# Reading the stationary weights of split fp32 matmuls with a step of two elements

## The chip, the cores and the metric

The kernel runs on one core of a Trainium2 chip. The metric is the device time of one execution in microseconds (us), the median of several runs. Engines are named as in the profile: PE is TensorE's matmul, PEld TensorE's loading of the stationary operand (the weights that stay in the array while the moving operand streams past), DVE is VectorE, ACT ScalarE, POOL GpSimd, SP the engine whose queue issues the DMAs.

## The reference: what is computed

Two layers of an encoder over 256 positions of width 2048, everything in fp32. Layer 0 mixes tokens with a gated MLP, layer 1 with grouped-query attention; after each comes a gated FFN with a convolution of width 3. A vector `c` gives shifts, scales and gates.

```
for i in range(2):
    sh1, sc1, gt1, sh2, sc2, gt2 = split(silu(c) @ w_ada[i] + b_ada[i], 6)
    h = rmsnorm(x, g_norm[i, 0]) * (1 + sc1) + sh1
    y = gmlp(h) if i == 0 else gqa(h)        # 2048->4096, 2048->2048 / 2048->3072, 2048->2048
    x = x + gt1 * y
    h = rmsnorm(x, g_norm[i, 1]) * (1 + sc2) + sh2
    a = conv3(h @ f_w_up[i])                 # 2048 -> 11264
    g, val = split(a, 2)
    x = x + gt2 * ((gelu(g) * val) @ f_w_down[i])   # 5632 -> 2048
return rmsnorm(x, g_final)
```

## The kernel before

Activations lie transposed in SBUF: 128 features on the partitions, 256 positions along them. Every weight is streamed once from HBM through SP's queue, in runs of up to 128 x 2048 fp32 (`raw_tile`). To multiply in TensorE's fast fp32 format (fp32r) without losing fp32's accuracy, each operand is split in two: `hi` is the value rounded to fp32r, `lo` the rest. For weights `weight()` does this in pieces of `HW` = 1024 columns: ACT writes `hi` (line 186), VectorE writes `lo` (line 187). Activations are split into `hhi`/`hlo` (`make_h`) or `fhi`/`flo` (`split_f`); their rows are `S + STEP` = 264 elements apart, of which 256 are used, so that the rows begin at staggered addresses.

`weight()` returns a function `cols(c, n)`, which gives the `hi` and `lo` views of n columns from column c. There are two kinds of use:

- `prod_b` takes blocks of 128 columns as the *stationary* operand (`cols(c, P)`) and the 256 positions of an activation as the moving one. It issues three matmuls, `hi` x `xhi`, `hi` x `xlo`, `lo` x `xhi`, all through line 203; before each of them TensorE loads the 128 columns. Its outputs are named pu and po (gated MLP), pw (attention's output), pfa, pfc and pf (FFN up), pd (FFN down).
- The products pv, pk and pq take 512 columns of weights as the *moving* operand and an activation as the stationary one.

TensorE executes its matmuls in program order; loops over output blocks are outside, loops over the 128-blocks of the reduction inside, accumulating in PSUM. While it works on one run of weights, SP, ACT and VectorE prepare the next ones (five buffers each of raw runs, `hi` and `lo`). VectorE also computes the vector-matrix product with `w_ada` (`ada`, line 138) between its other work, and the convolution. The order of all engines is made by a scheduler when the program is built.

The host lays the weights out for this before the launch (`_layout`): the 128 columns of block 0, then those of block 1, and so on.

Of the kernel before, what the change touches and what calls it, by code (L numbers as in the profile page):

```python
# [15 lines left out]
P = 128  # L16
# [31 lines left out]
def kernel(  # L48
# [32 lines left out]
    def raw_tile(name):  # L81
        return raws.tile([P, 2048], F32, tag="raw", name=name)
# [87 lines left out]
    def pump():  # L170
        state["credit"] += state["rate"]
        while state["credit"] >= 1.0 and queue:
            state["credit"] -= 1.0
            pump_one()

    def weight(src, ncol):
        pump()
        cnt[0] += 1
        w = raw_tile(f"w{cnt[0]}")
        Q.dma_start(w[:, :ncol], src)  # L180
        his_, los_ = [], []
        for c in range(0, ncol, HW):
            n = min(HW, ncol - c)
            hi = his.tile([P, HW], F32R, tag="hi", name=f"hi{cnt[0]}_{c}")
            lo = los.tile([P, HW], F32R, tag="lo", name=f"lo{cnt[0]}_{c}")
            A.copy(hi[:, :n], w[:, c:c + n])  # L186
            V.tensor_tensor(out=lo[:, :n], in0=w[:, c:c + n], in1=hi[:, :n].bitcast(F32), op=ALU.subtract)  # L187
            his_.append(hi)
            los_.append(lo)

        ready = list(pend)
        pend.clear()
        for fn in ready:
            fn()

        def cols(c, n):
            k, o = divmod(c, HW)
            return his_[k][:, o:o + n], los_[k][:, o:o + n]

        return cols  # L200
# [503 lines left out]
def _cols(a, *lead):  # L704

    n = a.shape[-1] // P
    a = a.reshape(*a.shape[:-1], n, P)
    return np.moveaxis(a, -1, 0)


def _nblock(w):

    K, N = w.shape
    return w.reshape(K // P, P, N // P, P).transpose(2, 1, 0, 3).reshape(N // P, P, -1)


def _rope_tables():
    rows = S // 64
    row_pos = np.repeat(np.arange(rows), 64).astype(np.float32)
    col_pos = np.tile(np.arange(64), rows).astype(np.float32)  # L720
    inv = (np.float32(10000.0) ** (-np.arange(0, 64, 2, dtype=np.float32) / np.float32(64))).astype(np.float32)
    ar, ac = row_pos[:, None] * inv, col_pos[:, None] * inv
    cos = np.concatenate([np.cos(ar), np.cos(ar), np.cos(ac), np.cos(ac)], 1)
    sin = np.concatenate([-np.sin(ar), np.sin(ar), -np.sin(ac), np.sin(ac)], 1)
    f = lambda a: a.astype(np.float32).reshape(TC, P, P).transpose(1, 0, 2)
    return f(cos), f(sin)


def _layout(inp):
    a = {k: np.asarray(v) for k, v in inp.items()}  # L730
    o = {}
    o["xT"] = a["x"][0].T.reshape(NB, P, S).transpose(1, 0, 2)
    o["cT"] = _cols(a["c"][0])
    o["wada"] = a["w_ada"].transpose(0, 2, 1).reshape(DEPTH, 6 * NB, P, D)
    o["bada"] = _cols(a["b_ada"])
    o["gn"] = _cols(a["g_norm"].reshape(DEPTH * 2, D))
    o["gf"] = _cols(a["g_final"])
    win = a["a_w_in"][0]
    o["wv"] = win[:, D:].reshape(NB, P, D)
    o["wu"] = _nblock(win[:, :D])  # L740
    o["gv"] = _cols(a["a_g_v"][0])
    o["wsT"] = a["a_w_s"][0].transpose(2, 0, 1).reshape(P, NB * P)
    o["bs"] = a["a_b_s"][0].reshape(NB * P)
    o["wout"] = _nblock(a["a_w_out"][0])
    wq = a["b_w_qkv"][0]
    o["wqkv0"] = np.concatenate([wq[:, 2048:3072], wq[:, :512]], 1).reshape(NB, P, 1536)
    o["wqkv1"] = wq[:, 512:2048].reshape(4, 4, P, 3, 512).transpose(3, 0, 2, 1, 4).reshape(3, 4, P, 2048)
    swap = lambda g: g.reshape(2, 2, 32)[:, ::-1].reshape(P)
    o["gq"] = np.stack([a["b_g_q"][0], swap(a["b_g_q"][0])])
    o["gk"] = np.stack([a["b_g_k"][0], swap(a["b_g_k"][0])])  # L750
    o["wo"] = (a["b_w_o"][0].reshape(2, 8, P, 8, 2, P).transpose(0, 3, 2, 4, 1, 5).reshape(2, 8, P, 2048))
    up = a["f_w_up"].reshape(DEPTH, NB, P, 2, NPAIR, P)
    outer = lambda u: u.transpose(0, 1, 2, 4, 3, 5).reshape(DEPTH, -1, P, KO * S)
    o["wup0"] = np.concatenate([outer(up[:, :H, :, :, :KO]), outer(up[:, :, :, :, KO:2 * KO])], 1)
    o["wup1"] = up[:, :, :, :, 2 * KO:].transpose(0, 4, 3, 2, 1, 5).reshape(DEPTH, NPAIR - 2 * KO, 2, P, D)
    o["wup2"] = up[:, H:, :, :, :KO].transpose(0, 4, 2, 3, 1, 5).reshape(DEPTH, KO, P, 2 * (NB - H) * P)
    o["cw"] = _cols(a["f_conv_w"])
    o["cb"] = _cols(a["f_conv_b"])
    dn = a["f_w_down"].reshape(DEPTH, NPAIR, P, NB, P)
    parts, b = [], 0  # L760
    for nk in PARTS:
        parts.append(dn[:, b:b + nk].transpose(0, 2, 3, 1, 4).reshape(DEPTH, P, NB * nk * P))
        b += nk
    o["wdn"] = np.concatenate(parts, 2)
    o["ident"] = np.eye(P, dtype=np.float32)
    o["cos"], o["sin"] = _rope_tables()
    return {k: np.ascontiguousarray(v) for k, v in o.items()}

# [22 lines left out]
```

## Time and profile before

| | |
|---|---|
| median of 3 runs | 2161.05 us (2160.24 to 2161.67) |
| profiled execution | 2160.85 us |
| its span, first to last instruction | 2158.9 us |
| PE busy | 2086.4 us, 16,328 matmuls |
| PEld busy | 2020.9 us, 16,328 loads |
| DVE busy | 1704.8 us |
| ACT busy | 1020.2 us |
| mean granted clock of TensorE | 0.983 |

A busy time is the time in which at least one instruction of that row is under way. Matmuls and loads overlap each other, and the end of a matmul is modelled in the profile; the distance from one start to the next is what is measured. The granted clock is a share of TensorE's full 2.4 GHz.

### The profile page before, as it was taken

Reading aid. Unit: us, or ns where it says so; the run is one execution under the profiler, and the core shown is the slowest. Engines: PE = TensorE matmul, PEld = TensorE weight load, DVE = VectorE, ACT = ScalarE, POOL = GpSimd, SP = SyncE. Lnnn points to the kernel's source line nnn. Section 1 sums busy time; section 2 is a strip of 40 time slices with the busy share of each in tenths; the row PEclk is TensorE's granted clock in tenths of the full one; section 3 lists DMA queues with packets and bytes.
Section 4 is the critical chain, followed back from the end, with each engine's and each line's share of the span. In section 5 each row is a group of like instructions: output and inputs, shape, how many; then the busy total and the mean of one; then the engine's idle time right before and its main releaser. Section 6 shows DMA issues by size and latency. Waiting matters only on the chain.

```text
span 2158.9 us, 39151 instructions
## 1 busy us (share of the span) xinstructions
PE 2086.4 (97%) x16328; PEld 2020.9 (94%) x16328; DVE 1704.8 (79%) x2291; ACT 1020.2 (47%) x1501; POOL 16.6 (1%) x15
## 2 busy tenths in 40 slices
PE   6889998999999999999999999899999999999997
PEld 4669998999999999999988789899999999999997
DVE  8989888899988989889985677876978666655665
ACT  3354443446544554345455554443753455434542
POOL 0000000000000000000000000000000000000000
PEclk8999999999999999999999999899999999999999
DMA  9999987995798889888966346578558655555542
GB/s 381 400 378 372 347 334 278 335 363 206 286 362 332 330 320 344 336 324 316 341 244 214 117 176 236 218 283 296 197 179 318 229 191 180 192 182 189 178 159 94
DMA packets 85137, 580.62 MB, mean 269 GB/s; under 512 B 9952, under 2 KB 11488, under 8 KB 25056
## 3 DMA queue, kind: packets, MB, share of 16 engines
q1 hardware_dynamic: 84960, 578.12, 72.0%
q8 instruction: 128, 2.10, 0.4%
q14 instruction: 49, 0.40, 0.0%
HBM read 575.99 MB, written 2.10 MB: 268 GB/s over the span
## 4 chain that ended last, share of the span: by engine, by line
PE 55%; issue 36%; DVE 7%; ACT 1%; POOL 0%; DMA 0%; SPq 0%; POOLq 0%; DVEq 0%; ACTq 0%
PE pf L203 18%; PE pd L203 11%; PE po L203 4%; PE pw L203 4%; PE pu L203 4%; PE pfc L203 4%; PE pk L203 3%; DVE ada L138 3%; PE pq L203 3%; DVE lo L187 2%; PE pfa L203 2%; PE pqo L507 1%; PE pv L203 1%; PE psc L478 0%; ACT hi L186 0%
## 5 line engine op out<-in xcount | busy, mean ns | idle before, releaser
L186 ACT CAST hi<-w 128x1024 fp32r<-128x1024 f32 x740 | 741.0, 1009 | 916.6 <-PE pf L203 348.5
L187 DVE TENSOR_TENSOR lo<-w,hi 128x1024 fp32r<-128x1024 f32 x740 | 857.9, 1169 | 329.9 <-ACT hi L186 326.3
L203 PE MATMUL pf<-hhi_f,hi 128*128 128x256 f32 x2144 | 604.4, 282 | 0.0
L203 PE MATMUL pf<-hhi_f,lo 128*128 128x256 f32 x2144 | 601.2, 280 | 0.0
L203 PE MATMUL pf<-hlo_f,hi 128*128 128x256 f32 x2144 | 600.9, 280 | 0.0
L138 DVE CUSTOM_DVE_ANT_0 ada<-ada,cond_bc,bada 128x2048 f32<-128x2048 f32 x192 | 449.2, 2345 | 42.6 <-DMA ada<-in_wada 42.5
L203 PEld LDWEIGHTS pf<-hlo_f,hi 128*128 128x128 f32 x2144 | 404.8, 189 | 0.0
L203 PEld LDWEIGHTS pf<-hhi_f,lo 128*128 128x128 f32 x2144 | 404.3, 189 | 0.0
L203 PEld LDWEIGHTS pf<-hhi_f,hi 128*128 128x128 f32 x2144 | 403.8, 188 | 0.0
L203 PE MATMUL pd<-fhi_f,lo 128*128 128x256 f32 x1408 | 394.7, 281 | 0.0
L203 PE MATMUL pd<-flo_f,hi 128*128 128x256 f32 x1408 | 393.3, 280 | 0.0
L203 PE MATMUL pd<-fhi_f,hi 128*128 128x256 f32 x1408 | 391.1, 279 | 0.0
L203 PEld LDWEIGHTS pd<-fhi_f,hi 128*128 128x128 f32 x1408 | 264.8, 189 | 0.0
L203 PEld LDWEIGHTS pd<-fhi_f,lo 128*128 128x128 f32 x1408 | 264.7, 188 | 0.0
L203 PEld LDWEIGHTS pd<-flo_f,hi 128*128 128x128 f32 x1408 | 264.6, 188 | 0.0
L203 PE MATMUL pfc<-hhi_f,hi 128*128 128x256 f32 x448 | 125.3, 281 | 0.0
L203 PE MATMUL pfc<-hlo_f,hi 128*128 128x256 f32 x448 | 125.0, 281 | 0.0
L203 PE MATMUL pfc<-hhi_f,lo 128*128 128x256 f32 x448 | 124.4, 281 | 0.0
L571 DVE SCALAR_TENSOR_TENSOR t<-pf,cw,t 128x255 f32<-128x255 f32 x240 | 101.7, 474 | 0.0
L203 PEld LDWEIGHTS pfc<-hlo_f,hi 128*128 128x128 f32 x448 | 84.2, 188 | 0.0
L203 PEld LDWEIGHTS pfc<-hhi_f,lo 128*128 128x128 f32 x448 | 84.2, 189 | 0.0
L203 PEld LDWEIGHTS pfc<-hhi_f,hi 128*128 128x128 f32 x448 | 84.1, 188 | 0.0
(187 smaller groups left out, 2838.3 us busy)
## 6 DMA issues: line engine op xcount, KB each, us to landing
ada<-in_wada SPq DMA_DIRECT2D x192, 1024.0 KB, 6.6
w<-in_wup SPq DMA_DIRECT2D x134, 1024.0 KB, 4.9
w<-in_wdn SPq DMA_DIRECT2D x64, 1024.0 KB, 4.9
w<-in_wup SPq DMA_DIRECT2D x48, 896.0 KB, 5.9
w<-in_wdn SPq DMA_DIRECT2D x32, 768.0 KB, 4.6
w<-in_wv SPq DMA_DIRECT2D x16, 1024.0 KB, 6.9
w<-in_wu SPq DMA_DIRECT2D x16, 1024.0 KB, 7.2
w<-in_wout SPq DMA_DIRECT2D x16, 1024.0 KB, 5.2
```

What stands on the lines that cost most here:

```text
L138: V.tensor_tensor_reduce(out=w, in0=w, in1=cond_bc, op0=ALU.mult, op1=ALU.add, scale=1.0, scalar=bada[:, l, m:m + 1], accum_out=mod[:, l, ...
L186: A.copy(hi[:, :n], w[:, c:c + n])
L187: V.tensor_tensor(out=lo[:, :n], in0=w[:, c:c + n], in1=hi[:, :n].bitcast(F32), op=ALU.subtract)
L203: T.matmul(out, lhsT=a, rhs=b, start=start, stop=stop, skip_group_check=True)
L507: T.matmul(po, lhsT=va[:, kc, g * P:(g + 1) * P], rhs=ps_[h][:, kc, :], start=kc == 0, stop=kc == TC - 1)
L571: V.scalar_tensor_tensor(out=o[:, to], in0=a[:, frm], scalar=cw[:, l, tap, n:n + 1], in1=o[:, to], op0=ALU.mult, op1=ALU.add)
```

## The change

The stationary views of `prod_b` are read with a step of two elements instead of one. Two neighbouring blocks of 128 columns (256 columns) are laid by turns by the host: column 0 of the first block, column 0 of the second, column 1 of the first, and so on (`_pairs`), in all seven arrays that feed `prod_b`. `cols` then takes, for n = 128, the pair of blocks in which c lies and every second element of it, beginning with element 0 for the even block and element 1 for the odd one. Views of 512 columns and their arrays are left as they are, and so is everything about the activations, whose padding was there before.

```
         def cols(c, n):
             k, o = divmod(c, HW)
+            if n == P:
+                o, q = o // (2 * P) * (2 * P), o // P % 2
+                return [t[:, o:o + 2 * P].rearrange("p (n q) -> p q n", q=2)[:, q, :] for t in (his_[k], los_[k])]
             return his_[k][:, o:o + n], los_[k][:, o:o + n]
...
+def _pairs(w):
+    return w.reshape(*w.shape[:-1], -1, 2, P).swapaxes(-1, -2).reshape(w.shape)
...
+    for k in ("wu", "wout", "wo", "wup0", "wup1", "wup2", "wdn"):
+        o[k] = _pairs(o[k])
```

On all five engines the program has the same instructions in the same order as before, with the same tiles and sizes; the only difference is the address pattern of the stationary operand.

## Rows read from the trace of the kernel before

**Rows 1.** The page's head: the span, and TensorE's busy us, share and instructions.

```profile
span 2158.9 us, 39151 instructions
PE 2086.4 (97%) x16328; PEld 2020.9 (94%) x16328; DVE 1704.8 (79%) x2291; ACT 1020.2 (47%) x1501; POOL 16.6 (1%) x15
```

**Rows 2.** Stretches: us; busy us (count) of PE, PEld, DVE, ACT, POOL; clock; DMA.

```profile
200.00:300.00 100.00, 100.00 (x850) 100.00 (x850) 88.30 (x103) 45.31 (x60) 0.00 (x0) 1.00 0.91 356
1000.00:1100.00 100.00, 99.60 (x845) 99.52 (x844) 95.35 (x131) 47.26 (x67) 0.00 (x0) 1.00 0.90 333
1600.00:1700.00 100.00, 100.00 (x851) 100.00 (x850) 72.33 (x76) 38.47 (x40) 0.00 (x0) 1.00 0.77 282
```

**Rows 3.** Groups of TensorE's instructions: shapes, count, busy us, mean ns.

```profile
L203 PE MATMUL pf<-hlo_f,hi 128*128 128x256 f32 x2144 | 600.9, 280 | 0.0
...
L203 PE MATMUL pd<-flo_f,hi 128*128 128x256 f32 x1408 | 393.3, 280 | 0.0
...
L203 PE MATMUL pfc<-hlo_f,hi 128*128 128x256 f32 x448 | 125.0, 281 | 0.0
...
L203 PE MATMUL pw<-flo_o,hi 128*128 128x256 f32 x256 | 71.9, 281 | 0.0
...
L203 PE MATMUL pu<-hlo_a,hi 128*128 128x256 f32 x256 | 71.6, 280 | 0.0
...
L203 PE MATMUL po<-flo_y,hi 128*128 128x256 f32 x256 | 71.5, 280 | 0.0
...
L203 PE MATMUL pfa<-hlo_f,hi 128*128 128x256 f32 x224 | 63.7, 286 | 0.0
...
L478 PE MATMUL psc<-kT,qT 128*128 128x256 f32 x64 | 14.5, 379 | 0.0
```

**Rows 4.** The same view of TensorE's loads: an ordinary one, a transpose's.

```profile
L203 PEld LDWEIGHTS pf<-hlo_f,hi 128*128 128x128 f32 x2144 | 404.8, 189 | 0.0
...
L472 PEld LDWEIGHTS pqo<-ident,rotq 128*128 128x128 f32 x32 | 3.9, 140 | 0.9
```

**Rows 5.** Timeline, end of the last FFN: start us, us, instruction.

```profile
2142.73 0.28 PE L203 MATMUL pd<-fhi_f,hi 128*128 128x256 f32 x1
...
2143.90 0.28 PE L203 MATMUL pd<-flo_f,hi 128*128 128x256 f32 x1
2144.03 0.28 PE L203 MATMUL pd<-fhi_f,lo 128*128 128x256 f32 x1
...
2145.09 0.28 PE L203 MATMUL pd<-fhi_f,lo 128*128 128x256 f32 x1
```

**Rows 6.** Timeline of attention: 512 columns; fp32 scores (16 merged).

```profile
1258.19 0.39 PE L203 MATMUL pq<-hi,hlo_b 128*128 128x512 f32 x1
...
1259.81 0.39 PE L203 MATMUL pq<-hi,hhi_b 128*128 128x512 f32 x1
...
1262.83 3.62 PE L478 MATMUL psc<-kT,qT 128*128 128x256 f32 x16
...
1266.52 0.39 PE L203 MATMUL pq<-hi,hlo_b 128*128 128x512 f32 x1
...
1271.64 0.39 PE L203 MATMUL pq<-hi,hhi_b 128*128 128x512 f32 x1
```

**Rows 7.** Timeline of attention after a pause, and that stretch's granted clock.

```profile
1249.42 0.63 PE L203 MATMUL pq<-lo,hhi_b 128*128 128x512 f32 x1
...
1251.56 0.63 PE L203 MATMUL pq<-hi,hhi_b 128*128 128x512 f32 x1
...
1249.42:1252.41 2.99, 2.99 (x8) 0.50 0.00 0
```

**Rows 8.** Timeline of loads: matmuls of one column (8 merged).

```profile
2145.09 0.97 PEld L246 LDWEIGHTS pm_fin<-mean_w,acc_fin 128*128 128x128 f32 x8
```

**Rows 9.** Timeline of the gated MLP: a matmul, and the next loads.

```profile
158.67 0.28 PE L203 MATMUL pu<-hhi_a,lo 128*128 128x256 f32 x1
159.39 0.63 PEld L366 LDWEIGHTS pg<-ws,v 128*128 128x128 f32 x5 [0.65 <-DVE v L328]
```

## What the change will do to the time, and why

> **What bounds the kernel now.** I read the page's head first [rows 1]: TensorE is busy for 2086.4 of 2158.9 us. Then I cut the span into stretches of 100 us [rows 2]. In 15 of the 20 from 100 to 2100 us TensorE is busy for all or nearly all of the time at a granted clock of 1.00, which is the upper of its two levels, 2.4 GHz, and has 845 to 851 matmuls in each, whether VectorE is busy for 72 us or 95 and whether the DMA engines are at 0.77 or 0.91. The rest is the start, which waits for loads of weights, the attention part, and the last norm. So over most of the span the time is the number of matmuls times the step from one to the next, and only something that alters that step, or makes TensorE wait, can alter the time.
>
> The reader should take the step from starts, not from durations: a matmul is listed with 280 ns [rows 3] and a weight load with 189 [rows 4], but they overlap. From 2142.73 to 2145.09 us 21 matmuls of 256 columns start, so the step is 2.36 us / 20 = 118.0 ns [rows 5]. At 2.4 GHz 256 columns are 106.7 ns. What are the other 11.3 ns?
>
> Three kinds of row say. With 512 columns and the same 128 loaded, 23 matmuls start from 1266.52 to 1271.64 us: 5.12 / 22 = 232.7 ns; eight others take 1.62 / 7 = 231.4 [rows 6]. For fp32 operands, whose 256 columns take two cycles each, the step is (3.62 - 0.38) / 15 = 216.0 ns, 2.7 over the 213.3 of the clock [rows 3, 6]. And at the lower level (granted 0.50, 1.2 GHz) 512 columns take 2.14 / 5 = 428 ns against 426.7 [rows 7]. So there is a fixed part of about 2.7 ns, and a loss that appears only where a 4-byte moving column is taken in each 2.4 GHz cycle. Its size is the slope: (232.7 - 118.0) / 256 = 0.448 ns a column instead of 0.4167, that is 8.0 ns in 256 columns (7.5%). 2.7 + 8.0 of the 11.3 are named; **0.6 ns is left that the loading of weights could be guilty of** (1.9 ns with the 231.4). A loss caused by loads would be the same for 256 and 512 columns, since one load lies beside each; it doubles instead. A matmul that starts at 158.67 us has no load beside it, since the loads pause for 0.65 us until 159.39, and it is listed with 0.28 us as well [rows 9]; ends are modelled, so that is a hint, not a proof.
>
> **The change, part by part.** It removes nothing, adds no instruction and moves none. The host lays the columns of two neighbouring 128-column blocks by turns, in arrays of the same size, so the DMAs carry the same bytes in the same pieces. The split into hi and lo takes whole 1024-column runs and doesn't see the order: ACT's and VectorE's instructions cost what they cost. Nothing waits for anything new. `cols` serves `prod_b` alone with n == P; the wide reads (pv, pk, pq) stay as they are, and wv and wqkv aren't laid anew. What is left is one edit, the address step of the stationary read, from 4 to 8 bytes, in 2144 + 1408 + 448 + 256 + 256 + 256 + 224 = 4992 products of three matmuls each [rows 3]: 14,976 loads. **One nanosecond on each step is therefore 15.0 us**, 0.7%.
>
> What does a load cost now? Where the matmul is one column wide, loads set the pace: eight of them in 0.97 us, the last 0.19 long, so (0.97 - 0.19) / 7 = 111.4 ns each [rows 8]. A transpose's load is listed with 140 ns, the others with 189 [rows 4]: 49 ns less, near the 53 that 128 cycles are. So the ordinary 4-byte load seems to take a column in two cycles, 106.7 ns for 128, and with 111.4 that fits. Beside matmuls of 256 columns such a load is hidden, but with only 118.0 - 111.4 = 6.6 ns to spare. That cover hides the edit, and decides it.
>
> No stationary read in this trace has a step above one, so its price is bounded from the nearest rows. Below: if the load as it is costs the matmul the 0.6 to 1.9 ns left over and the new order removes that, 9 to 28 us are gained; all of 6.6 ns, down to the load's own pace, would be 99 us. Above: the load would now cover 1024 bytes in 106.7 ns, the very pace in bytes at which the moving operand loses 7.5%. With that loss it takes 111.4 x 1.075 = 119.8 ns, 1.8 over the step now: +27 us. If each element now cost what two cost before, it takes 111.4 + 106.7 = 218 ns: +100 ns a step, +1502 us. Between them I take zero: the loss follows the moving operand's columns, and the stationary operand is still read at half their rate, as the fp32 moving operand is, which shows no loss.
>
> [...]
>
> The sum: 2160.85 us, the profiled execution's time (its span of 2158.9 and 1.95 around it), plus zero. The median of the runs shown is 2161.05, 0.2 above it. **Forecast: 2161 us, no change.**
>
> **The rivals.** (a) *The stepped load becomes the bound*, slower. Place: every one of the 14,976 steps. It decides from 6.6 ns more per load. At the moving operand's loss it gives 2161 + 27 = 2188 us; a load that touches twice the span and so gets in the moving read's way twice as often would give 0.6 to 1.9 ns more per step, 2170 to 2189. For it: the small slack, and that the pace in bytes is exactly the one that loses. Against: a loss of less than 6% of a load stays hidden. (b) *Each stepped element pays double*, 3663 us. Against it: the load takes two cycles a column already, which leaves room for a slower fetch.
>
> (c) *Faster*: loading and streaming now walk through memory at the same pace in bytes, where before the moving read passed the load again and again; if the loss comes from two reads meeting in one place, they meet less. For it: single steps differ though the instructions are alike, as 0.13 us from 2143.90 to 2144.03 among a mean of 0.118 [rows 5], so something about addresses counts. Against: the doubling with 512 columns. Price: 9 to 28 us, the middle is 2142 us. The far end, 2062, isn't to be had: VectorE is busy for 95 us of a stretch in the first FFN at the present step [rows 2], so there it would become the bound at about 5%.
>
> [...]
>
> **How the numbers follow.** No change 0.35, since the one resource altered is hidden now; (a) 0.31; (b) 0.08; (c) 0.26. With a bound of 0.2% (4.3 us, about what a measurement of this kernel tells from no change) that is faster 0.26, same 0.35, slower 0.39: no single case beats "no change", though slower as a whole is a little likelier. The range must hold (a) with its 2188 and (c) with its 28 us, and more, as both are estimates: 2105 to 2205. Outside are (b), 0.06 for a gain beyond 56 us, and 0.06 for an (a) of more than 44: 0.20 in all. If no change is right, the time lies within 2157 to 2165.
>
> **What the next profile would show.** If I am right, the step at the end of the last FFN is 118 ns again, busy stretches hold 845 to 851 matmuls, loads are listed with 189 ns, and the 512-column steps, which the edit doesn't touch, are 231 to 233. (a) shows as loads listed longer and a step of 119 to 120 or more, in all of pf, pd, pu, po and pw alike; (b) as some 460 matmuls in 100 us, with ACT and VectorE idle in between; (c) as a step below 117.5 with TensorE still busy throughout. I am wrong if the 8.0 ns are not the moving operand's own, if the slack of 6.6 ns isn't one because the two reads share something, or if the step alters what the uneven single steps come from.

## The result and the profile after

| | before | after |
|---|---|---|
| median, each of 4 runs side by side | 2161.36 us | 2193.7 us (2189.87 to 2196.61) |
| profiled execution, its span | 2160.85, 2158.9 us | 2193.63, 2191.7 us |
| ratio to before, 95% interval | | 1.0149 [1.0132, 1.0167] |

The change makes the kernel slower by 1.5%. The time lies in the range given, but the forecast of no change was wrong; it is rival (a) that came, with 2188 us forecast for it.

The head of the page answers to [rows 1]: as many instructions, and TensorE busy for 34.1 us longer (2120.5 against 2086.4), which is the whole difference of the spans, 32.8 us, and a little more (TensorE is idle for 1.3 us less).

```profile
span 2191.7 us, 39151 instructions
PE 2120.5 (97%) x16328; PEld 2055.1 (94%) x16328; DVE 1708.2 (78%) x2291; ACT 1019.8 (47%) x1501; POOL 16.6 (1%) x15
```

The same three stretches as in [rows 2]:

```profile
200.00:300.00 100.00, 100.00 (x832) 100.00 (x831) 86.99 (x102) 44.35 (x59) 0.00 (x0) 1.00 0.91 347
1000.00:1100.00 100.00, 100.00 (x834) 100.00 (x833) 92.53 (x124) 46.79 (x67) 0.00 (x0) 1.00 0.89 326
1600.00:1700.00 100.00, 100.00 (x834) 100.00 (x833) 76.53 (x95) 43.68 (x53) 0.00 (x0) 1.00 0.71 257
```

TensorE is busy for all of each stretch at the same granted clock of 1.00, but has 832 to 834 matmuls in it instead of 845 to 851: 100 us / 832 to 834 = 119.9 to 120.2 ns from one to the next. No wait has appeared, and over the span no other engine is nearer to being full (VectorE 78% against 79%). Averaged over the starts of `prod_b` in the trace, the step is 118.1 ns before and 120.4 ns after; 2.3 ns x 14,976 loads is 34 us, as TensorE's busy time grew. By the span it is 32.8 us / 14,976 = 2.2 ns. Nothing else is to be explained.

The groups of TensorE's matmuls, and of its loads (answering to [rows 3] and [rows 4]; line 203 is now 207):

```profile
L207 PE MATMUL pf<-hlo_f,hi 128*128 128x256 f32 x2144 | 607.4, 283 | 0.0
...
L207 PE MATMUL pd<-flo_f,hi 128*128 128x256 f32 x1408 | 396.7, 283 | 0.0
...
L207 PE MATMUL po<-flo_y,hi 128*128 128x256 f32 x256 | 72.5, 283 | 0.0
```

```profile
L207 PEld LDWEIGHTS pf<-hlo_f,hi 128*128 128x128 f32 x2144 | 421.8, 197 | 0.0
...
L207 PEld LDWEIGHTS pq<-lo,hhi_b 128*128 128x128 f32 x96 | 18.1, 188 | 3.8
```

A stepped load is listed with 197 ns where the same load had 189. That is a hint only: the load of pq, which the change doesn't touch, is listed with 188 ns here and had 193 before. The wide products, timeline of attention (answering to [rows 6]): 35 matmuls of 512 columns start from 1284.72 to 1292.63 us, 7.91 / 34 = 232.6 ns, as before.

```profile
1284.72 0.40 PE L207 MATMUL pq<-lo,hhi_b 128*128 128x512 f32 x1
...
1292.63 0.40 PE L207 MATMUL pq<-hi,hlo_b 128*128 128x512 f32 x1
```

So the loss is in the steps of `prod_b` and nowhere else: by their starts all seven outputs have 119.9 (pd) to 120.8 ns (pf), where they had 117.5 to 118.4. What makes the step longer is not in this trace. Two theories stood:

- **A**: the stepped load itself takes about 118 to 120 ns and sets the pace wherever the matmul beside it is shorter.
- **B**: the stepped read gets in the way of the moving read, and adds about 2 ns to a matmul of any length.

### The profile page after: what moved, and what is told of

Its sections match the earlier page's. It is cut to its first block, busy times and chain, and to the rows that moved or that the text cites. A ratio compares the mean times of both kernels' runs of the same rounds, so it can differ in the third digit from the quotient of the medians.

```text
span 2191.7 us, 39151 instructions
## 1 busy us (share of the span) xinstructions
PE 2120.5 (97%) x16328; PEld 2055.1 (94%) x16328; DVE 1708.2 (78%) x2291; ACT 1019.8 (47%) x1501; POOL 16.6 (1%) x15
## 4 chain that ended last, share of the span: by engine, by line
PE 55%; issue 36%; DVE 7%; ACT 1%; POOL 0%; DMA 0%; SPq 0%; POOLq 0%; DVEq 0%; ACTq 0%
PE pf L207 18%; PE pd L207 11%; PE po L207 4%; PE pw L207 4%; PE pu L207 4%; PE pfc L207 4%; DVE ada L138 3%; PE pk L207 3%; PE pq L207 3%; DVE lo L187 2%; PE pfa L207 2%; PE pqo L511 1%; PE psc L482 0%; PE psc L504 0%; ACT hi L186 0%
## 5 line engine op out<-in xcount | busy, mean ns | idle before, releaser
L207 PE MATMUL pf<-hhi_f,hi 128*128 128x256 f32 x2144 | 611.5, 285 | 0.0
L207 PE MATMUL pf<-hlo_f,hi 128*128 128x256 f32 x2144 | 607.4, 283 | 0.0
L207 PEld LDWEIGHTS pf<-hlo_f,hi 128*128 128x128 f32 x2144 | 421.8, 197 | 0.0
L207 PEld LDWEIGHTS pf<-hhi_f,hi 128*128 128x128 f32 x2144 | 421.0, 196 | 0.0
L207 PEld LDWEIGHTS pf<-hhi_f,lo 128*128 128x128 f32 x2144 | 419.8, 196 | 0.0
L207 PE MATMUL pd<-fhi_f,hi 128*128 128x256 f32 x1408 | 397.0, 283 | 0.0
L207 PEld LDWEIGHTS pd<-fhi_f,hi 128*128 128x128 f32 x1408 | 276.3, 197 | 0.0
L207 PEld LDWEIGHTS pd<-flo_f,hi 128*128 128x128 f32 x1408 | 275.4, 196 | 0.0
L207 PEld LDWEIGHTS pd<-fhi_f,lo 128*128 128x128 f32 x1408 | 275.1, 196 | 0.0
```

The lines of the kernel that those rows point to most:

```text
L207: T.matmul(out, lhsT=a, rhs=b, start=start, stop=stop, skip_group_check=True)
```

## The experiments

**1. A micro kernel of TensorE alone (`m1_paces`).** It computes nothing of the reference: 96 matmuls of each kind follow each other, from operands that lie in SBUF, with loads of step 1, 2 and 4 and moving operands of several lengths.

```
def stat(w, b, s):                       # block of 128 columns, read with step s
    o, q = b // s * (s * P), b % s
    return w[:, o:o + s * P].rearrange("p (n q) -> p q n", q=s)[:, q, :]
...
for i in range(96):
    T.matmul(ps[:, :n], lhsT=stat(w, i % 16, s), rhs=h[:, i % 8, :n])
```

> Not the reference: 96 matmuls in a row of each kind, on weights and activations of the inputs, nothing else. Two theories for the 2.2 ns per step. A (the load sets the pace): a load read with a step of two takes about 120 ns instead of 111 and shows wherever the matmul is shorter. Steps from start to start: 64 columns 111 ns with step one, 120 with step two; 256 columns 118 and 120; 288 columns 0.448 x 288 + 2.7 = 131.7 with both; 512 columns 232 with both. B (the stepped read gets in the moving read's way more): 64 columns 111 with both; 256 columns 118 and 120; 288 columns 132 and 134; 512 columns 232 and 234 to 236. Step four has no row yet: A with a price per distance gives up to 218 ns wherever the matmul is shorter, A with a price per element none more than step two. A moving operand read with a step of two shows whether it, too, is slowed by distance: up to 230 ns if so, 118 if not.

Stretches from the start of the first to the start of the last of 96, so 95 steps each (columns: us, PE busy and count with what reaches into the stretch, granted clock, DMA). In order: 256 columns with step 1, 2, 4; 64 columns with step 1, 2, 4; 128 columns with step 1, 2.

```profile
25.84:37.08 11.24, 11.24 (x97) 1.00 0.00 0
37.20:48.60 11.40, 11.40 (x97) 1.00 0.01 1
48.72:70.89 22.17, 22.17 (x98) 1.00 0.00 1
71.12:87.89 16.77, 16.77 (x97) 0.61 0.01 1
88.10:108.37 20.27, 20.27 (x97) 0.50 0.00 0
108.58:130.72 22.14, 22.14 (x96) 0.50 0.00 1
222.02:232.59 10.57, 10.57 (x96) 1.00 0.01 2
232.71:243.94 11.23, 11.23 (x97) 1.00 0.01 1
```

Divided by 95: 118.3, 120.0 and 233.4 ns with 256 columns, and 111.3 and 118.2 ns with 128, where a matmul is so short that only the load sets the pace (matmuls of one column follow each other in 111.4 ns as well [rows 8]). **So the stepped load by itself takes 6.9 ns longer**, which is all of the slack that a 256-column matmul left it. That is A's mechanism, but not A's size: 118.2 ns is no more than the 118.3 that the step had, and beside 256 columns it is 120.0. The 64-column runs fell into the lower level of the clock (granted 0.50), and so don't test what they were made for. They show something else: at that level step two costs nothing (20.27 / 95 = 213.4 ns; with step one the part of the stretch after the clock fell has 213 too), while step four takes 233.1 ns, nearly the 233.4 at granted 1.00. So in these runs the price is one in ns, not in cycles of TensorE. An estimate says why step two is free there: 512 moving columns took 428 ns at granted 0.50 [rows 7], 0.836 ns each, and two such times for each of 128 columns are 214 ns, longer than the 118.2 of the stepped load.

The longer moving operands of this kernel come from a tile whose rows all begin at the same address modulo 256 bytes as the stationary blocks (with step two every other block begins 4 bytes further). From start to start again, in order: the last 60 steps of 512 columns with step 1 (the series began at the lower clock); the 95 steps of 512 columns with step 2 and with step 4; the last 60 steps of 288 columns with step 1 and with step 2.

```profile
141.48:155.08 13.60, 13.60 (x61) 1.00 0.00 1
155.31:177.48 22.17, 22.17 (x97) 1.00 0.00 1
177.72:200.04 22.32, 22.32 (x97) 1.00 0.00 0
248.72:256.62 7.90, 7.90 (x62) 1.00 0.00 0
261.42:269.42 8.00, 8.00 (x62) 1.00 0.00 0
```

13.60 / 60 = 226.7 ns with step 1 and 22.17 / 95 = 233.4 with step 2; with 288 columns 131.7 and 133.3. **Here a step of two costs 6.7 ns beside 512 columns and 1.6 beside 288**, although the matmul is longer than a load of 118.2 ns in both. A asked for no difference, B for 2 to 4 ns and for 2. So at these starts the stepped load does make the matmul beside it longer, as B has it. There is one series of each; the 226.7 ns come again in experiment 5, the 233.4 only here.

**2. How the price goes on (`m3_lines`).** The same kernel with 128 columns and steps 1 to 8, then longer moving operands with step 1 and 2.

```
-    T.matmul(ps[:, :64], lhsT=stat(w, i % 16, s), rhs=h[:, i % 8, :64])
+    T.matmul(ps[:, :128], lhsT=stat(w, i % 16, s), rhs=h[:, i % 8, :128])       # s = 1, 2, 3, 4, 8
+    T.matmul(ps[:, :n], lhsT=stat(w, i % 16, s), rhs=g[n][:, i % 8, :n])        # n = 320, 384, 512; s = 1, 2
```

> Not the reference: 96 matmuls in a row of each kind. Loads of step one, two, three, four and eight beside matmuls of 128 columns, where the load sets the pace; then 320, 384 and 512 columns, rows 8 elements further apart than they are long so that all relative addresses occur, with loads of step one and two. If a load pays per 16 bytes touched (1.8 to 1.85 ns each, as 64 x 1.85 = 118 and 128 x 1.82 = 233 have it): 111, 118, about 175, 233, 233. If it pays by distance: 111, 118, 175, 233, 466. A (pace): 320, 384 and 512 columns alike for step one and two, about 146, 175 and 232. B (meeting): step two is slower by 1.6 ns or more in each of them.

Stretches of 95 steps again: 128 columns with step 1, 2, 4, 8.

```profile
26.54:37.09 10.55, 10.55 (x97) 1.00 0.00 0
37.20:48.43 11.23, 11.23 (x97) 1.00 0.01 1
68.16:90.42 22.26, 22.26 (x96) 0.50 0.00 1
90.66:113.44 22.78, 22.78 (x97) 0.50 0.00 0
```

111.1, 118.2, 234.3 and 239.8 ns (the last two at granted 0.50; step three lay there with 213.3 ns, as long as step two's 213.4 at that clock in experiment 1, and tells nothing). Step eight costs hardly more (2%) than step four. So here the distance isn't what is paid for. What doubles from two to four and not again is the number of 16-byte lines that 128 elements touch: 32, 64, 128 and 128. 118.2 / 64 = 1.85 and 234.3 / 128 = 1.83 ns a line. The moving operand pays nearly the same: [rows 6] give 232.7 / 128 = 1.82 ns, and 256 columns read with a step of two as *moving* operand (in the first micro kernel) take 226.7 ns, as long as 512 that lie together. With step one a load touches 32 lines, 59 ns at that price, half of the 111.1 that it takes. That 16 bytes are the unit is an estimate from these times, and nothing else here shows it.

The longer moving operands here have rows 8 elements further apart than they are long, so that their starts vary as in the kernel. 384 columns with step 1 and 2, then 512:

```profile
143.63:160.34 16.71, 16.71 (x98) 1.00 0.00 1
160.51:177.25 16.74, 16.74 (x96) 1.00 0.00 0
177.43:199.68 22.25, 22.25 (x97) 1.00 0.00 1
199.91:222.03 22.12, 22.12 (x97) 1.00 0.00 1
```

Divided by 95: 175.9 and 176.2 ns, 234.2 and 232.8; with 320 columns the last two thirds of the steps have 147.1 and 146.7. With mixed starts the step of two is free on average beside these 320 to 512 columns. **B is refuted as a price on every matmul**: it asked for 1.6 ns or more in all of these. It is not refuted as a price at certain starts, which the equal starts of experiment 1 show (233.4 against 226.7 ns).

**3. Half of the change alone (`e_down_only`).** Only wdn is laid in pairs and read stepped: 4,224 of the 14,976 loads.

```
-    for k in ("wu", "wout", "wo", "wup0", "wup1", "wup2", "wdn"):
+    for k in ("wdn",):
...
-            if n == P:
+            if n == P and pair:          # pair is True in weight() for wdn alone
```

> Only the FFN's down projection is read with a step of two (4,224 of the 14,976 loads); the other six arrays are laid and read as before. A and B alike: 2.2 ns x 4,224 = 9 us more than before, 0.43%, and pd alone has a step of 120.3 ns, with pf at 118. If the time instead came from somewhere that the loads share (the order of the work, the arrival of weights), it would be 0 or the whole 33 us.

2168.81 us against 2159.16, ratio 1.0043 [1.0029, 1.0057]: 9.3 us by the ratio, for 4,224 loads, is 2.2 ns each. A stretch with pu and po, and one in the last FFN of which two thirds are pd:

```profile
200.00:300.00 100.00, 100.00 (x850) 1.00 0.92 354
1900.00:2000.00 100.00, 100.00 (x840) 1.00 0.51 182
```

850 matmuls where nothing is stepped, as in [rows 2], and 840 in the other; steps of pd run at 119.9 ns by their starts (117.9 before), those of pf stay at 118.3. The cost goes with the stepped loads and stays there.

**4. Only the host's layout (`e_layout_only`).**

```
-            if n == P:
+            if n == 0:                   # pairs are laid, but read with step one
```

> Half of the change: the host lays the columns of two blocks by turns in all seven arrays, but the stationary blocks are read with a step of one, so that they hold mixed columns. Both theories: no change against before, 2160 us within 0.2%, since only the address step counts. If it is slower by 10 us or more, the data's arrangement or the random state of the weights would count.

2159.27 against 2159.94 us, ratio 1.0 [0.9991, 1.0009]. The layout costs and brings nothing; the read is all.

**5 and 6. Without the padding of the activations (`e_before_nopad`, `e_after_nopad`).** The unevenness of single steps in [rows 5] had made me suspect addresses. Here the rows of the activations lie 256 elements apart instead of 264, in the kernel before and in the changed one.

```
-STEP = 8
+STEP = 0
```

> The kernel before with the activations' rows 256 elements apart instead of 264, so that moving and stationary reads always begin at the same relative address. It gives the other half of a two by two with the next run. If relative addresses count for the moving read, it is slower than before by up to 2 ns a step, 2161 to 2191 us.

> The changed kernel with rows 256 apart. A: the load of about 120 ns sets the pace whatever the moving read does below that, so the time stays within 0.3% of the changed kernel, about 2194 us. B: the cost of missing padding and that of the step add up: 2194 plus whatever the run without padding before lost.

Before: 2172.62 against 2159.16 us, ratio 1.006 [1.0046, 1.0074]; changed: 2185.22, ratio 1.0118 [1.0104, 1.0132], 0.4% below the changed kernel with padding (0.3% by the two ratios), at the border of the 0.3% that A allows and far from the 2207 us of B. Two stretches of the first kernel, pu with po and then nine tenths pd, and one of the second, pu with po:

```profile
200.00:300.00 100.00, 100.00 (x843) 1.00 0.92 352
1600.00:1700.00 100.00, 100.00 (x850) 1.00 0.76 281
```

```profile
200.00:300.00 100.00, 100.00 (x836) 1.00 0.91 349
```

Without padding the steps become regular. In the kernel before, 48 steps of pf take 5760 ns again and again, 120.0 each; 48 of pd take 5653, 117.8 each. The moving rows of pf begin at the same address modulo 256 bytes as the stationary block, those of pd 64 bytes further. So **a step depends on where the two reads begin relative to each other**, with loads of step one too. In the changed kernel every step is 120.0, at either of these starts. These 120.0 ns are 1.8 above the load's own pace. Padding, which is worth 13 us before, costs 7 to 8 us after the change. Of these, 5.7 are the 960 wide products, which take 226.7 ns at these starts (24 of pk in 5440 ns) instead of 232.6.

**7. The starts by themselves (`m2_phases`).** 48 matmuls of 256 columns for each of 24 starts of one moving row, with step 1 and then step 2.

```
+    for s in (1, 2):
+        for ph in (0, 2, 4, 6, 8, 12, 16, 20, 24, 28, 32, ..., 48, ..., 64, ..., 112, 128):   # in elements
+            for i in range(48):
+                T.matmul(t, lhsT=stat(w, i % 16, s), rhs=hw[:, ph:ph + 256])
```

> Not the reference: 48 matmuls of 256 columns in a row for each of 24 offsets of the moving operand's start (0 to 128 elements) against the stationary blocks, with loads of step one and then of step two. A (a load of about 118 to 120 ns sets the pace): with step two all offsets give 118 to 121, and with step one they spread from about 114 (the moving read alone, as fast as the 226.7 ns of 512 columns imply) to 120. B (the two reads meet in memory): with step two the offsets spread at least as widely as with step one, and some give no more than step one does. If there is an offset at which step one stays near 114 to 115, it is worth 3 ns x 14,976 = 45 us in the kernel before.

Timeline (start us, us, instruction; 48 merged to a row; sap is step 1, sbp step 2, the last letter the start: h 80, i 96, j 112, o 192, s 256 bytes after the block's start). From one series' start to the next one's are 48 steps.

```profile
54.01 5.92 PE L45 MATMUL saph<-hw,w 128*128 128x256 f32 x48
59.77 5.92 PE L45 MATMUL sapi<-hw,w 128*128 128x256 f32 x48
65.53 5.60 PE L45 MATMUL sapj<-hw,w 128*128 128x256 f32 x48
70.97 5.85 PE L45 MATMUL sapk<-hw,w 128*128 128x256 f32 x48
...
93.70 5.62 PE L45 MATMUL sapo<-hw,w 128*128 128x256 f32 x48
99.15 5.88 PE L45 MATMUL sapp<-hw,w 128*128 128x256 f32 x48
...
116.18 5.92 PE L45 MATMUL saps<-hw,w 128*128 128x256 f32 x48
121.94 5.87 PE L45 MATMUL sapt<-hw,w 128*128 128x256 f32 x48
...
190.51 5.82 PE L45 MATMUL sbph<-hw,w 128*128 128x256 f32 x48
196.17 5.93 PE L45 MATMUL sbpi<-hw,w 128*128 128x256 f32 x48
...
230.76 5.93 PE L45 MATMUL sbpo<-hw,w 128*128 128x256 f32 x48
236.53 5.91 PE L45 MATMUL sbpp<-hw,w 128*128 128x256 f32 x48
```

With step one: 5.76 / 48 = 120.0 ns at 96 and at 256 bytes, 5.44 / 48 = 113.3 at 112, 5.45 / 48 = 113.5 at 192, and most others from 117 to 120. Starts that occur twice modulo 256 bytes agree within 0.6 ns, but for 16 and 272 bytes (116.8 and 118.9): the start says much of the step, not all. With step two 192 bytes give 5.77 / 48 = 120.2; 20 of the 24 starts lie between 119.7 and 121.2, the other four between 117.9 and 119.1. The spread of 6.7 ns has shrunk to 3.4, as A has it and not B; but at 80 bytes step two gives less than step one (117.9 against 120.0), which B allows for and no pace of the load explains. There are 6.7 ns to gain with step one, and they are lost with step two.

The kernel's eight starts, 0 to 224 bytes in steps of 32, have a mean of 117.8 ns here with step one and 120.2 with step two, so this kernel gives the 2.3 ns again. If the load did no more than keep each step from falling below its own 118.2 ns, the mean would be 118.7. By this estimate **its pace alone accounts for 0.9 of the 2.4 ns**; the rest appears only beside a 256-column matmul.

**8 and 9. The good start in the whole kernel (`e_start192`, `e_start192_step2`).** All activation rows lie 256 elements apart and begin 192 bytes (modulo 256) behind the stationary block; the loads have step one, and in the second kernel step two.

```
-STEP = 8
+STEP = 0
+SH = 48
+SF = 32
...
+        cur["f"].tile([P, SF], F32, tag="sf", name=f"sf_{name}", bufs=1)     # moves fhi, flo
...
-        hts["hi"] = hbuf.tile([P, NB, S + STEP], F32R, ...)[:, :, :S]          # and the same for lo
+        t = hbuf.tile([P, NB * S + 64], F32R, tag=f"h{k}", ...)               # k: hi, lo
+        hts[k] = t[:, SH:SH + NB * S].rearrange("p (j t) -> p j t", t=S)
```

> The kernel before (step one) with all activation rows 256 elements apart and placed so that every moving read of prod_b begins 192 bytes, modulo 256, behind the start of its stationary block. The row of matmuls at that offset had a step of 113.3 ns, so A (moving read 113, load 111, the longer sets the pace) gives a step of 113.3 instead of 118.1 and 4.8 x 14,976 = 72 us less than before, about 2089 us, some us more where VectorE, busy for 95 of 100 us in the first FFN, can't follow. If the 113.3 ns hold only for one moving row read again and again, it stays at 2150 to 2161.

> The same placement with the change's step of two. A: the stepped load of 118 to 120 ns sets the pace, so the step is 120.0 and the time about 2185 us, as without padding; nothing of the 72 us is gained, and the change costs 96 us here instead of 32. B (the step costs by its meetings with the moving read, 1.6 to 2.2 ns wherever it stands): 113.3 + 2 = 115 ns, about 2120 us.

With step one: 2123.15, 2148.40, 2120.55 and 2122.94 us, median 2123.04 against 2159.94, ratio 0.9861 [0.9796, 0.9926]. **This beats both kernels**, though by half of what was expected, and one of its four runs gained only 12 us. With step two: 2185.42 us, ratio 1.0115 [1.01, 1.013], as A said (2185; B 2120). Stretches, with step one and then with step two:

```profile
200.00:300.00 100.00, 100.00 (x852) 1.00 0.92 355
500.00:600.00 100.00, 100.00 (x852) 1.00 0.70 263
1600.00:1700.00 100.00, 100.00 (x885) 1.00 0.77 285
2000.00:2100.00 100.00, 100.00 (x885) 1.00 0.42 146
```

```profile
200.00:300.00 100.00, 100.00 (x836) 1.00 0.91 347
1600.00:1700.00 100.00, 100.00 (x835) 1.00 0.74 271
```

In layer 1's FFN 885 matmuls lie in 100 us, with those that reach into it; from start to start they take 113.3 ns, the pace of the micro kernel. In most of layer 0 there are 852 (48 steps of pf take 5653, 117.8 each), with the same relative addresses. Neither the starts nor the layer explain this difference, nor does a wait, since single steps lie between 116 and 120 ns. The first blocks of pu run at the faster pace, until one step of 202 ns at 181.04 us; here are 41 steps of pu before it and 133 behind it:

```profile
176.39:181.03 4.64, 4.64 (x43) 1.00 1.00 410
181.35:197.02 15.67, 15.67 (x136) 1.00 1.01 421
```

4.64 / 41 = 113 ns and 15.67 / 133 = 118 ns. Each stretch of `prod_b` that nothing interrupts keeps the pace with which it begins: 6,316 steps from 352.6 to 1096.4 us have 117.8 ns and 5,469 from 1487.3 to 2107.0 us have 113.3; behind the interruptions in attention pw has now the one, now the other. What picks the pace isn't shown. Some 7,700 steps are 4.4 ns longer than the good pace, 34 us in all, which is the distance to the expected 2089 us; that was missed by an assumption, that the addresses fix the step. With step two all of it is 120 ns, and here the change costs 62 us instead of 32.

## Why the prediction was wrong

**What held.** The frame did: the time is the number of matmuls times the step, one nanosecond is 15.0 us, nothing else moves, and the wide products stay at 232.6 ns. So did the slack of 6.6 ns as what is at stake: a load takes 111.3 ns and a step 118, and the stepped load's 6.9 ns more use it up. The 2.4 GHz that it reckons with stand here as an estimate, with one column a cycle: 512 columns in 428 ns at granted 0.50 [rows 7] are 1.196 a ns, so 2.39 at 1.00.

**The step that failed** is "Between them I take zero: the loss follows the moving operand's columns, and the stationary operand is still read at half their rate, as the fp32 moving operand is, which shows no loss". The load does lose, 6.9 ns (118.2 against 111.3) where zero was taken, and beside 256 columns the step goes to 120. Columns were the wrong unit, if the price goes by lines of 16 bytes, as the times of experiment 2 suggest. By that estimate, and with the 106.7 ns for 128 loaded or 256 moving columns that the prediction reckons with, a load of step two reads half the columns in a time, but each 16-byte line holds only two of them, so it touches one line in the time of two of its columns, 1.67 ns, just as the moving operand does with four columns of half that time. The fp32 operand, which I took as the like case, touches one in 3.3 ns (213.3 / 64, of a step measured at 216.0 [rows 6]): that is the pace of a load of step *one* (106.7 / 32, of a measured 111.3), not of step two. The right comparison stood a few sentences ahead, in the upper bound ("the very pace in bytes at which the moving operand loses 7.5%"), and its 119.8 ns compare with 118.2 for the load alone and 120.0 beside a matmul of 256 columns. Against (a) I set that "a loss of less than 6% of a load stays hidden"; the loss is 6.2% alone (118.2 / 111.3), at the border, and a further 1.8 ns appear beside a matmul. Those stood in no term of the sum: it had the load either hidden or setting the pace. (a) does name a meeting of the two reads, for 0.6 to 1.9 ns, but as another way to the loss and not on top of a slower load. The signs that were named for (a), 119 to 120 ns or more in all of pf, pd, pu, po and pw alike and loads listed longer, are what the profile shows.

**The size of (a)** was 1.8 ns a step, 27 us; measured are 2.2 ns, 32.8 us. That it came so near is partly luck: its 119.8 ns were to be the load's own pace, which is 118.2, and the rest appears only beside a matmul.

**Rival (b)**, 218 ns, is excluded by the 197 ns listed and the 832 to 834 matmuls. Something of its size comes with step four (233.4 ns).

**Rival (c)** had the wrong sign for this change and half a right reason. Where the two reads begin does count, as the starts of experiment 7 (113.3 to 120.0 ns) and the 512 columns of experiment 1 (226.7 and 233.4) show, and the price of that was set too low: not 0.6 to 1.9 ns were left for it, but up to 6.7 (120.0 against 113.3). That the two reads meet in one place is my reading of it; no run shows the meeting itself. The split of the 11.3 ns into 2.7 fixed and 8.0 of the moving operand's own was read from one mixture of addresses: at the best fixed starts 256 columns take 113.3 ns (192 bytes) and 512 take 226.7 (equal starts, experiments 1 and 5), the double, 0.443 ns a column with no fixed part. The doubling that I took for proof that loads are not guilty is no such proof. But with a stepped load the good start brought nothing: the load takes 118.2 ns by itself, and the step stays at 120 (48 steps in 5.77 us at 192 bytes in experiment 7; 835 or 836 matmuls in 100 us in experiment 9).

**Open** is why a load of 118.2 ns makes the step 120.0 beside 256 columns at nearly every start, and whether that has the same cause as the 6.7 ns beside 512 columns; what picks between 117.8 and 113.3 ns where the starts are equal, which may also be what gave one execution 2148 us, of which there is no trace; and the price of step three.

## What to carry to other kernels

Count what an operand touches in 16-byte lines per time, and not in columns alone: as an estimate, 1.77 to 1.85 ns a line fit both operands here (226.7 / 128 for the moving one, 118.2 / 64 for the load). 4-byte weights read with a step of two load in 118.2 ns here instead of 111.3, which costs 2% of each step beside 256 columns (120.4 against 118.1 ns) and, with mixed starts, nothing beside the 320, 384 and 512 columns that were measured (232.8 against 234.2 ns with 512). When a hidden resource is within 6% of becoming the bound, "still hidden" is not a forecast; measure it alone, with matmuls so short that it sets the pace, and then beside the matmul that is to hide it, since here the two together took 120.0 ns, where the load alone took 118.2 and the step with the ordinary load 118.3. Before the layout of weights is changed, try where the rows of the moving operand begin: it was worth 37 us here, in a kernel in which TensorE was busy all the time, though the pace that it gave was not the same throughout.

## What was not expected of the hardware

- The step of a 256-column fp32r matmul depends on the relative start of its two operands: 120.0 ns at the same start modulo 256 bytes and 117.8 at 64 (`e_before_nopad`), 113.3 to 114 at 112 and 192 (`m2_phases`).
- The price of a stepped load is one in ns in these runs: at granted 0.50 step two is free (213.4 ns, and 213 with step one), and step four takes 233.1 ns there and 233.4 at 1.00.
- A load of 118.2 ns beside a much longer matmul still costs: at equal starts a step of two makes a 512-column matmul 233.4 ns instead of 226.7; with mixed starts it costs nothing (232.8 against 234.2).
- Two steady paces, 117.8 and 113.3 ns, appear in one execution at equal relative starts (`e_start192`). A stretch keeps its pace for thousands of steps; the pace changed only where the row of matmuls had been interrupted.
